# Summing the squares of all six norms by TensorE products in four groups of 32 rows

## The chip, the cores and the metric

The kernel runs on one core of one Trainium2 chip. The metric is the device time of one execution in microseconds. The core has TensorE (products into PSUM), VectorE, ScalarE, GpSimd and SyncE, which issues nearly all transfers; each takes its own queue in order, and they wait for each other by semaphores.

## The reference

Two layers on 1024 tokens with 1024 channels, cut to what matters here. Each layer first takes the root-mean-square norm of a token over its channels and modulates it; the convolution layer also has a LayerNorm over channels inside. All of these need a sum of squares over the channels of each token.

```python
def _rms(x, g):
    xf = x.astype(jnp.float32)
    y = xf * lax.rsqrt(jnp.mean(xf * xf, axis=-1, keepdims=True) + EPS)
    return (y * g.astype(jnp.float32)).astype(x.dtype)

# layer 0 (convolution module), layer 1 (multi-scale pooling mixer); for each:
sh, sc, gt = jnp.split((s_lat @ w_mod[i] + b_mod[i])[:, None, :], 3, axis=-1)
h = _rms(x, norm_g[i]) * (1.0 + sc) + sh
x = x + gt * mixer(h)
# layer 0:  a, b, g = split(h @ w_in);  y = depthwise_conv31(a * sigmoid(b)) + db
#           y = silu(_layernorm(y)) * silu(g);  return y @ w_out
# layer 1:  v, g = split(h @ w_in);  y = grouped(window_means(v) - v) * scale
#           return (y * silu(g)) @ w_out
```

## The kernel before

Activations lie channels by tokens: a channel tile is 128 partitions, and the 1024 tokens are two halves of 512 columns (`h` = 0, 1). A half thus has eight tiles of 128x512. Weights and activations of the large products are split into a high and a low part (`load_split`, `hi_part`, `lo_part`, L162 to L198), and `mm3` (L200) makes three products per tile, with one accumulation over eight tiles in a PSUM bank (`gemm`, L208).

The stages in program order are: norm of x for each half (`norm_x`, L327) with the adaLN vectors of layer 0 made on VectorE between them (`mod_block`, L344); the input products of layer 0 and their gates (`pf`, `pg`, `ps`); adaLN vectors of the rest by `gemv` (L291); the depthwise convolution with 31 taps, per channel tile and half, either on VectorE (L484) or as ScalarE products and GpSimd adds (L471, L472; `POOL_CT` lists GpSimd's tiles: two of eight in the first half, five of eight in the second); the gate products `psg` (L511); the LayerNorm of a half (`layernorm`, L529); the gating (`gate_norm`, L548); the output products `pso` with the residual (`out_half`, L575), which also forms the norm of the second layer (`h2_half`, L606); and layer 1 (`psv`, `psq`, `psy`, `psf`) in two parts.

Six norms sum squares over channels: x0, x1 (the inputs of layer 0), z0, z1 (the variance in the LayerNorm) and y0, y1 (the inputs of layer 1); the digit is the half. Two ways are in use:

- `squares` (L252), for x0, x1 and y1: ScalarE squares a tile (L259, L262), VectorE adds it into one 128x512 total (L266), and `rstd_rows` then sums the partitions of the total by four products, each with a 128x128 block of it as weights and one column of ones streamed (L234). For y1 the last tile is not added but goes through four products of its own.
- `square_sums` (L270), for z0, z1 and y0: ScalarE squares a tile (L275), and four products per tile add it into the four columns of a bank (L277).

Both leave the sums of 512 tokens as 128 partitions by 4 columns. `rstd_rows` (L225) then takes the mean and adds eps on ScalarE (L240), raises to -1/2 on GpSimd (L242), spreads each column into a diagonal on ScalarE (L247, four) and sums the diagonals with ones in one product (L248, `rb`), so that each partition holds the factor of each token. `sq` is a ring of two tiles for the squares.

The order on each engine is set by a planner that runs while the kernel is built: it takes instructions by priority as a simulated timeline makes them ready. `priority(-LATER)` puts a step ahead of all that is not marked so, `LATER * (1 + h)` puts the conv taps behind. `behind(...)` holds a step back in the queue until a named one has been queued; `gemm` uses it to keep a part of its products for the time in which a norm is on its way.

A float32 product appears in the trace as two loads of weights and two multiplies, so the four products of a tile are 8 and 8 instructions.

Of the kernel before, what the change touches and what calls it, by code (L numbers as in the profile page):

```python
# [9 lines left out]
F32 = mybir.dt.float32  # L10
F32R = mybir.dt.float32r
AF = mybir.ActivationFunctionType
# [41 lines left out]
def hybrid_kernel(ctx, tc, xT, vecs, wm, wk, cv_first, cv_w, cv_wo, pl_w, pl_grp, pl_wo, out):  # L54
# [3 lines left out]
    PS = ctx.enter_context(tc.tile_pool(name="ps", bufs=1, space=bass.MemoryType.PSUM))  # L58
    DR = ctx.enter_context(tc.tile_pool(name="dr", bufs=1, space=bass.MemoryType.DRAM))

    RINGS = {"w": 4, "raw": 4, "sg": 2, "sq": 2, "pr": 2, "vs": 1}
    WIDTH = {"E": 2 * NB, "Z": 2 * (NB + 2 * PAD), "sg": NB + 2 * PAD, "pr": NB}
    LATER = 1 << 20
    tc.cur_priority = 4 * LATER
# [31 lines left out]
    def axps(name):  # L96
        return bank("ax", name)
# [4 lines left out]
    def bl(j):  # L102
        return slice(j * P, (j + 1) * P)
# [118 lines left out]

    power_done, spread_done = [None], [None]

    def rstd_rows(total, name):  # L225


        sums, vp = total
        if vp is None:
            vp = axps(f"vp{name}")  # L230
            with priority(-LATER):
                for i, summed in enumerate(sums):
                    for j in range(4):
                        nc.tensor.matmul(  # L234
                            vp[:, j : j + 1], summed[:, bl(j)], ones[:, 0:1], start=i + j == 0,
                            stop=i == len(sums) - 1, skip_group_check=True,
                        )
        ve = S.tile([P, 4], F32, tag="ve", name=f"ve{name}", bufs=2)
        with priority(-LATER):
            nc.scalar.activation(ve, vp[:, 0:4], AF.Identity, scale=1.0 / D, bias=eps)  # L240
        rs = S.tile([P, 4], F32, tag="vr", name=f"vr{name}", bufs=2)
        power_done[0] = nc.gpsimd.tensor_tensor(out=rs, in0=ve, in1=mhalf[:, 0:4], op=ALU.pow)  # L242
        rb = axps(f"rb{name}")
        dg = half("sq", f"dg{name}")
        with priority(-LATER):
            for j in range(4):
                spread = nc.scalar.activation(dg[:, bl(j)], ident, AF.Copy, scale=rs[:, j : j + 1])  # L247
            done = nc.tensor.matmul(rb, ones, dg, start=True, stop=True)  # L248
        spread_done[0] = spread
        return rb, done  # L250

    def squares(xs, name, apart=False):  # L252

        total = half("vs", f"va{name}")
        sums = [total]

        def add(i):
            if i == 0:
                nc.scalar.activation(total, xs[i], AF.Square)  # L259
                return None  # L260
            sq = half("sq", f"sq{name}{i}")
            nc.scalar.activation(sq, xs[i], AF.Square)  # L262
            if apart and i == KT - 1:
                sums.append(sq)
                return None
            return nc.vector.tensor_tensor(out=total, in0=total, in1=sq, op=ALU.add)  # L266

        return (sums, None), add

    def square_sums(xs, name, vp):  # L270


        def add(i):
            sq = half("sq", f"sq{name}{i}")
            done = nc.scalar.activation(sq, xs[i], AF.Square)  # L275
            for j in range(4):
                nc.tensor.matmul(  # L277
                    vp[:, j : j + 1], sq[:, bl(j)], ones[:, 0:1], start=i + j == 0, stop=i == KT - 1,
                    skip_group_check=True,
                )  # L280
            return done

        return (None, vp), add

    def dot(w, out):

# [38 lines left out]
            load_next(xs[h][kt], xT[bl(kt), hs(h)])  # L325

    def norm_x(h):  # L327
        total, add = squares(xs[h], f"x{h}")
        for kt in range(KT):
            last = add(kt)  # L330
        return last, rstd_rows(total, f"x{h}")[0]
# [243 lines left out]
    def out_half(h, y1, ws, done, beside=None):  # L575
        group = len(ws)
        x1 = packed([f"Z{j}" for j in range(4)], f"xr{h}")
        for m in range(KT):
            nc.sync.dma_start(out=x1[m], in_=xT[bl(m), hs(h)])
        total, add = squares(x1, f"y{h}", True) if h else square_sums(x1, f"y{h}", axps("vpy0"))  # L580

        def finish(m, ps):
            nc.vector.scalar_tensor_tensor(  # L583
                out=x1[m], in0=ps, scalar=gt0[:, m : m + 1], in1=x1[m], op0=ALU.mult, op1=ALU.add
            )
            nc.sync.dma_start(out=x1d[m][:, hs(h)], in_=x1[m])
            add(m)

        pss = [mmps(f"pso{h}{m}") for m in range(group)]
        for i, kt in enumerate(CORD):  # L590
            for m in range(group):
                mm3(pss[m], cut(ws[m], bl(kt)), y1[i], i == 0, i == KT - 1)
        for m in range(group):
            finish(m, pss[m])
        for m in range(group, KT):
            with behind([] if m >= group + 2 else done if h == 0 else power_done):
                w = load_split(cv_wo[m], f"wo{h}{m}", eng=(nc.vector, nc.gpsimd)[h])
            if beside is not None:
                beside(m)
            ps = mmps(f"pso{h}{m}")  # L600
            for i, kt in enumerate(CORD):
                mm3(ps, cut(w, bl(kt)), y1[i], i == 0, i == KT - 1)
            finish(m, ps)
        return x1, total
# [279 lines left out]
```

## Time and profile before

| | us |
|---|---|
| median of 3 runs | 758.52 (757.62 to 759.13) |
| the profiled execution | 758.71 |
| its span, first to last instruction | 756.9 |
| TensorE busy | 724.2 (96%) |
| VectorE busy | 532.1 (70%) |
| ScalarE busy | 386.4 (51%) |
| GpSimd busy | 435.4 (58%) |
| chain that ended last | TensorE 70%, VectorE 14%, GpSimd 8%, ScalarE 3% |

PE is TensorE's multiplying, PEld its loading of weights, DVE VectorE, ACT ScalarE, POOL GpSimd, SPq the transfers that SyncE issues. The shares are averages over the whole span; what a stage is limited by is read from its own windows. "PEclk" is the clock granted to TensorE, as a share of 2.4 GHz.

### The profile page before, as it was taken

Reading aid. Unit: us, or ns where it says so; the run is one execution under the profiler, and the core shown is the slowest. Engines: PE = TensorE matmul, PEld = TensorE weight load, DVE = VectorE, ACT = ScalarE, POOL = GpSimd, SP = SyncE. Lnnn points to the kernel's source line nnn. Section 1 sums busy time; section 2 is a strip of 40 time slices with the busy share of each in tenths; the row PEclk is TensorE's granted clock in tenths of the full one; section 3 lists DMA queues with packets and bytes.
Section 4 is the critical chain, followed back from the end, with each engine's and each line's share of the span. In section 5 each row is a group of like instructions: output and inputs, shape, how many; then the busy total and the mean of one; then the engine's idle time right before and its main releaser. Section 6 shows DMA issues by size and latency. Waiting matters only on the chain.

```text
span 756.9 us, 9894 instructions
## 1 busy us (share of the span) xinstructions
PE 724.2 (96%) x3572; PEld 574.1 (76%) x3572; DVE 532.1 (70%) x724; ACT 386.4 (51%) x576; POOL 435.4 (58%) x377
## 2 busy tenths in 40 slices
PE   3899999999999999999989989999999999999998
PEld 1677786676768788778766768788888788888997
DVE  5997997889898941589969989671737364477321
ACT  5355556656613346876886676652414433334110
POOL 2000889999913438899998999763117413344232
PEclk9999999999999999999999989999999999999999
DMA  8882006466323441643650132445625610334132
GB/s 324 315 318 82 0 1 249 167 223 233 132 82 98 152 153 63 202 140 113 207 171 24 57 126 83 154 168 160 203 92 203 200 56 28 98 112 140 56 126 72
DMA packets 36481, 105.68 MB, mean 140 GB/s; under 512 B 4048, under 2 KB 6224, under 8 KB 36432
## 3 DMA queue, kind: packets, MB, share of 16 engines
q1 hardware_dynamic: 36432, 105.05, 40.8%
q8 instruction: 28, 0.46, 0.2%
q14 instruction: 21, 0.17, 0.1%
HBM read 92.45 MB, written 12.58 MB: 139 GB/s over the span
## 4 chain that ended last, share of the span: by engine, by line
PE 70%; DVE 14%; POOL 8%; ACT 3%; issue 2%; DMA 2%; SPq 0%; DVEq 0%; POOLq 0%; ACTq 0%
POOL z L472 8%; PE ps L201 4%; PE ps L203 4%; PE ps L202 4%; PE psf L202 4%; PE psf L203 4%; PE psf L201 4%; PE psv L203 3%; PE psv L202 3%; PE psv L201 3%; PE psq L202 3%; PE psq L201 3%; PE psq L203 3%; PE psg L203 3%; PE psg L201 3%; PE psg L202 3%
## 5 line engine op out<-in xcount | busy, mean ns | idle before, releaser
L472 POOL TENSOR_TENSOR z<-z,pr 128x512 f32<-128x512 f32 (+8 forms) x210 | 297.1, 1415 | 49.4 <-ACT pr L471 21.2
L471 ACT ACTIVATE pr<-y,VT 128x512 f32<-128x512 f32 (+8 forms) x210 | 150.2, 719 | 96.8 <-POOL z L472 90.2
L484 DVE SCALAR_TENSOR_TENSOR cv<-y,VT,cv 128x512 f32<-128x512 f32 (+12 forms) x261 | 175.4, 741 | 0.4
L770 DVE SCALAR_TENSOR_TENSOR xf<-psf,gt,xf 128x260 f32<-128x260 f32 (+1 forms) x24 | 13.2, 570 | 36.9 <-PE psf L203 31.4
L753 DVE SCALAR_TENSOR_TENSOR q<-psy,VT,q 128x260 f32<-128x260 f32 (+1 forms) x24 | 13.6, 571 | 31.9 <-PE psy L203 31.7
L242 POOL TENSOR_TENSOR vrx<-vex,mhalf 128x4 f32<-128x4 f32 x2 | 2.1, 1026 | 57.2 <-ACT vex L240 57.2
L567 DVE TENSOR_TENSOR z<-z,rbz 128x512 f32<-128x512 f32 x16 | 10.7, 680 | 28.9 <-PE rbz L248 28.9
L671 DVE TENSOR_TENSOR s<-v 128x535 f32<-128x535 f32 x8 | 12.3, 1536 | 19.5 <-ACT v L719 19.5
L675 DVE TENSOR_TENSOR s<-s 128x517 f32<-128x517 f32 (+5 forms) x24 | 20.9, 870 | 0.6
L559 ACT ACTIVATE gn<-z,VT 128x512 f32<-128x512 f32 x16 | 12.4, 777 | 14.6 <-DVE z L567 14.4
L287 DVE SCALAR_TENSOR_TENSOR wmb<-wmb,s_row 128x1024 f32<-128x1024 f32 x16 | 19.4, 1220 | 0.0
L583 DVE SCALAR_TENSOR_TENSOR xr<-pso,gt,xr 128x512 f32<-128x512 f32 x16 | 11.5, 741 | 10.7 <-PE pso L203 10.7
L299 PE MATMUL gv<-wk,srep 128*32 128x256 f32 x256 | 18.6, 388 | 0.0
L164 ACT CAST y<-q 128x504 fp32r<-128x504 f32 (+1 forms) x16 | 9.9, 618 | 16.8 <-DVE q L753 16.8
L169 DVE TENSOR_TENSOR y<-q,y 128x504 fp32r<-128x504 f32 (+1 forms) x16 | 13.9, 869 | 3.6 <-ACT y L164 3.6
L277 PEld LDWEIGHTS vpz<-ones,sqz 128*128 128x128 f32 x128 | 15.5, 191 | 0.7
L275 ACT ACTIVATE sqz<-z 128x512 f32<-128x512 f32 x16 | 9.8, 629 | 12.0 <-PE vpz L277 11.5
L202 PE MATMUL psy<-pd,grs 128*128 128x260 f32 (+1 forms) x48 | 15.3, 320 | 0.0
L203 PE MATMUL psy<-pd,grs 128*128 128x260 f32 (+1 forms) x48 | 15.3, 319 | 0.0
L201 PE MATMUL psy<-pd,grs 128*128 128x260 f32 (+1 forms) x48 | 15.1, 318 | 0.0
L277 PE MATMUL vpz<-ones,sqz 128*128 128x1 f32 x128 | 14.7, 245 | 0.0
L169 DVE TENSOR_TENSOR grs<-gr,grs 128x512 fp32r<-128x512 f32 x8 | 9.1, 1132 | 8.0 <-ACT grs L164 8.0
(2503 smaller groups left out, 2352.6 us busy)
## 6 DMA issues: line engine op xcount, KB each, us to landing
wk<-in_wk SPq DMA_DIRECT2D x32, 512.0 KB, 5.1
wmb<-in_wm SPq DMA_DIRECT2D x16, 512.0 KB, 6.4
wo<-in_cv_wo SPq DMA_DIRECT2D x16, 512.0 KB, 3.5
wp<-in_pl_wo SPq DMA_DIRECT2D x16, 512.0 KB, 3.5
wg<-in_cv_w SPq DMA_DIRECT2D x12, 512.0 KB, 3.7
wv<-in_pl_w SPq DMA_DIRECT2D x12, 512.0 KB, 3.4
wq<-in_pl_w SPq DMA_DIRECT2D x12, 512.0 KB, 3.5
x<-in_xT SPq DMA_DIRECT2D x16, 256.0 KB, 6.2
```

Of the source, the lines that this page charges most:

```text
L169: return eng.tensor_tensor(out=lo, in0=src, in1=hi.bitcast(F32), op=ALU.subtract)
L201: nc.tensor.matmul(ps, w[0], r[0], start=first, stop=False)
L202: nc.tensor.matmul(ps, w[0], r[1], start=False, stop=False)
L203: nc.tensor.matmul(ps, w[1], r[0], start=False, stop=last)
L277: nc.tensor.matmul(vp[:, j : j + 1], sq[:, bl(j)], ones[:, 0:1], start=i + j == 0, stop=i == KT - 1, skip_group_check=True,)
L287: nc.vector.scalar_tensor_tensor(out=w, in0=w, scalar=1.0, in1=s_row, op0=ALU.mult, op1=ALU.mult, accum_out=out)
L299: nc.tensor.matmul(ps[32 * q : 32 * q + 32, :256], srep[:, kt, :], w[:, 256 * q : 256 * q + 256], start=kt == 0, stop=kt == KT - 1,)
L471: nc.scalar.activation(pr[:, o], y[:, i], AF.Copy, scale=dw(k))
L472: nc.gpsimd.tensor_tensor(out=z[:, o], in0=z[:, o], in1=pr[:, o], op=ALU.add)
L484: nc.vector.scalar_tensor_tensor(out=a[:, o], in0=y[:, i], scalar=dw(k), in1=a[:, o], op0=ALU.mult, op1=ALU.add)
L675: nc.vector.tensor_tensor(out=s[:, :m], in0=s[:, :m], in1=s[:, step : step + m], op=ALU.add)
L753: mixed[0] = nc.vector.scalar_tensor_tensor(out=sg[m][:, piece], in0=ps, scalar=vcol(ct, V_PS), in1=sg[m][:, piece], op0=ALU.mult, op1=ALU ...
```

## The change

All six norms sum their squares by products, tile by tile, and `squares` with its total is gone. The product is turned round: a constant block of 32 columns, `onesd` (1/1024), is the weights, and the 128 columns of a quarter of the tokens are streamed; quarter j writes rows 32j to 32j+31 of the bank, so the four sums of 128 tokens stand as rows. `rstd_rows` copies these 128x128 values with eps added, turns them into 128x4 by a product with `sel` (one 1 in each of rows 0, 32, 64 and 96), and copies these 4 columns; the power is now inside the priority block.

```diff
-    RINGS = {"w": 4, "raw": 4, "sg": 2, "sq": 2, "pr": 2, "vs": 1}
+    RINGS = {"w": 4, "raw": 4, "sg": 2, "sq": 2, "pr": 2}
...
-    def rstd_rows(total, name):
-        sums, vp = total
-        if vp is None:
-            vp = axps(f"vp{name}")
-            with priority(-LATER):
-                for i, summed in enumerate(sums):
-                    for j in range(4):
-                        nc.tensor.matmul(
-                            vp[:, j : j + 1], summed[:, bl(j)], ones[:, 0:1], start=i + j == 0,
-                            stop=i == len(sums) - 1, skip_group_check=True,
-                        )
-        ve = S.tile([P, 4], F32, tag="ve", name=f"ve{name}", bufs=2)
+    def token_sums(ps, src, first, last):
+        for j in range(4):
+            nc.tensor.matmul(ps[32 * j : 32 * j + 32, :P], onesd[:, :32], src[:, bl(j)], start=first, stop=last)
+
+    def rstd_rows(vp, name):
+        row = S.tile([P, P], F32, tag="vrow", name=f"vrow{name}", bufs=1)
+        rs = S.tile([P, 4], F32, tag="vr", name=f"vr{name}", bufs=2)
         with priority(-LATER):
-            nc.scalar.activation(ve, vp[:, 0:4], AF.Identity, scale=1.0 / D, bias=eps)
-        rs = S.tile([P, 4], F32, tag="vr", name=f"vr{name}", bufs=2)
-        power_done[0] = nc.gpsimd.tensor_tensor(out=rs, in0=ve, in1=mhalf[:, 0:4], op=ALU.pow)
+            nc.scalar.activation(row, vp[:, :P], AF.Identity, bias=eps)
+            nc.tensor.matmul(vp[:, P : P + 4], row, sel, start=True, stop=True)
+            ve = S.tile([P, 4], F32, tag="ve", name=f"ve{name}", bufs=2)
+            nc.scalar.copy(ve, vp[:, P : P + 4])
+            power_done[0] = nc.gpsimd.tensor_tensor(out=rs, in0=ve, in1=mhalf[:, 0:4], op=ALU.pow)
...
-    def squares(xs, name, apart=False):
...
     def square_sums(xs, name, vp):
         def add(i):
             sq = half("sq", f"sq{name}{i}")
             done = nc.scalar.activation(sq, xs[i], AF.Square)
-            for j in range(4):
-                nc.tensor.matmul(
-                    vp[:, j : j + 1], sq[:, bl(j)], ones[:, 0:1], start=i + j == 0, stop=i == KT - 1,
-                    skip_group_check=True,
-                )
+            token_sums(vp, sq, i == 0, i == KT - 1)
             return done
-        return (None, vp), add
+        return vp, add
...
     def norm_x(h):
-        total, add = squares(xs[h], f"x{h}")
+        total, add = square_sums(xs[h], f"x{h}", axps(f"vpx{h}"))
...
-        total, add = squares(x1, f"y{h}", True) if h else square_sums(x1, f"y{h}", axps("vpy0"))
+        total, add = square_sums(x1, f"y{h}", axps(f"vpy{h}"))
```

## Rows read from the trace of the kernel before

**Rows 1.** The page: a busy line and TensorE's forty slices, in tenths.

```profile
PE 724.2 (96%) x3572; PEld 574.1 (76%) x3572; DVE 532.1 (70%) x724; ACT 386.4 (51%) x576; POOL 435.4 (58%) x377
...
PE   3899999999999999999989989999999999999998
```

**Rows 2.** Windows of 10 us: length, PE, PEld, DVE, ACT, POOL busy; PEclk; DMA.

```profile
40.00:50.00 10.00, 9.44 (x40) 7.35 (x41) 9.99 (x20) 5.62 (x9) 0.00 (x0) 1.00 1.04 411
440.00:450.00 10.00, 6.26 (x25) 4.76 (x24) 9.44 (x10) 7.80 (x13) 9.69 (x11) 0.85 0.32 104
```

**Rows 3.** Timeline, TensorE, first burst of y0 (start, us, engine, line, operation, count).

```profile
337.54 0.39 PE L202 MATMUL pso<-y102l,wo04h 128*128 128x512 f32 x1
337.77 1.84 PE L277 MATMUL vpy<-ones,sqy 128*128 128x1 f32 x16
...
339.79 0.40 PE L201 MATMUL pso<-y102h,wo04h 128*128 128x512 f32 x1
```

**Rows 4.** Timeline, TensorE, last burst of y0.

```profile
372.44 0.39 PE L202 MATMUL psg<-h12l,wg61h 128*128 128x512 f32 x1
372.67 0.95 PE L277 MATMUL vpy<-ones,sqy 128*128 128x1 f32 x8
...
373.80 0.39 PE L201 MATMUL psg<-h14h,wg61h 128*128 128x512 f32 x1
```

**Rows 5.** The chain that ended last: first burst of z0, last of z1.

```profile
268.22 1.68 PE vpz L277 x16
...
522.84 1.68 PE vpz L277 x16
```

**Rows 6.** Timeline, TensorE, first burst of the adaLN vectors.

```profile
122.50 0.40 PE L203 MATMUL ps<-h04h,wb4l 128*128 128x512 f32 x1
122.83 0.64 PE L299 MATMUL gv<-wk,srep 128*32 128x256 f32 x8
...
123.74 0.39 PE L202 MATMUL ps<-h04l,wb4h 128*128 128x512 f32 x1
```

**Rows 7.** Timeline, TensorE, channel sums of the first LayerNorm (some records are missing).

```profile
225.16 0.39 PE L203 MATMUL ps<-h16h,wb7l 128*128 128x512 f32 x1
225.47 1.92 PE L537 MATMUL mr<-z,onesd 128*32 128x512 f32 x14
...
227.65 0.39 PE L202 MATMUL ps<-h10l,wa7h 128*128 128x512 f32 x1
```

**Rows 8.** Window of 40 ns, adaLN instructions only (length; PE, PEld busy and count).

```profile
122.87:122.91 0.04, 0.04 (x4) 0.04 (x8) 0.00 (x0) 0.00 (x0) 1.00 0.50 205
```

**Rows 9.** Instructions of the adaLN tile: duration in ns, least, median, most.

```profile
L299 PEld LDWEIGHTS gv<-wk,srep x256: 106/109/110, 122.8 to 214.4; 128*32 128x32 f32 x128
```

**Rows 10.** Timeline, TensorE, two turning products of an adaLN vector.

```profile
141.51 0.39 PE L202 MATMUL ps<-h16l,wb4h 128*128 128x512 f32 x1
141.74 0.50 PE L308 MATMUL gv<-sel,row 128*128 128x4 f32 x4
...
142.43 0.39 PE L201 MATMUL ps<-h10h,wa4h 128*128 128x512 f32 x1
```

**Rows 11.** VectorE's adds for x0 and x1 (tile view); TensorE's timeline at 75.

```profile
L266 DVE TENSOR_TENSOR vax<-vax,sqx x14: 682/690/693, 6.8 to 57.4; 128x512 f32<-128x512 f32 x14
...
75.35 0.50 PE L202 MATMUL pg<-h10l,w00h 128*128 128x512 f32 x1 [1.16 <-DVE h10l L170]
```

**Rows 12.** ScalarE's diagonal blocks of the x norms (tile view, ns).

```profile
L247 ACT ACTIVATE dgx<-ident,vrx x8: 387/387/402, 17.2 to 64.2; 128x128 f32<-128x128 f32 x8
```

**Rows 13.** Timeline, TensorE, spreading product of y0; idle before it in brackets.

```profile
382.49 1.13 PE L248 MATMUL rby<-dgy,ones 128*128 128x512 f32 x2 [0.74 <-ACT dgy L247]
```

**Rows 14.** Timeline, ScalarE and GpSimd: conv taps of the second half, start and end.

```profile
282.15 0.63 ACT L275 ACTIVATE sqz<-z 128x512 f32<-128x512 f32 x1 [4.17 <-PE vpz L277]
...
285.07 2.66 POOL L472 TENSOR_TENSOR z<-z,pr 128x512 f32<-128x512 f32 x2 [13.47 <-ACT pr L471]
...
484.68 3.96 POOL L472 TENSOR_TENSOR z<-z,pr 128x499 f32<-128x499 f32 x3
```

More of the change, by code (lines that the diff above doesn't have):

```diff
@@ L250, in rstd_rows @@
         return rb, done
-    def squares(xs, name, apart=False):
[L254 to L268, printed above, removed]
     def square_sums(xs, name, vp):
```

## The prediction

> **What bounds the kernel now.** I read the busy shares and the forty slices first: TensorE is busy in nearly every slice, VectorE, ScalarE and GpSimd are not [rows 1]. So a saved microsecond counts where TensorE is the one behind, and I looked for the stretches where it is not. In the windows TensorE has small gaps near the front, where VectorE is full, and one of 3.7 us near 445, with a lower clock in that window (0.85) [rows 2]. Everywhere else I treat TensorE time as the time of the kernel. Then I read, on TensorE's own timeline, what each way of summing squares costs.
>
> **The price of the old products.** A sum by `ones[:, 0:1]` loads a 128x128 block of squares as weights and streams one column, four times for one channel tile. Ordinary products start every 0.23 us, so a burst's price is the distance between the starts of its neighbours, less two ordinary steps (0.46). Two tiles in one burst: 337.54 to 339.79 is 2.25, less 0.46, 1.79 us [rows 3]. One tile: 372.44 to 373.80, 1.36 less 0.46, 0.90 us [rows 4]. Both z norms run as four bursts of two tiles, eight bursts in all, of which the first and the last stand in [rows 5]; y0 runs as two bursts of two and four of one, of which [rows 3, 4] show one each. x1 has one burst of one tile's size after VectorE has added its eight squares; y1 has two, because its last tile is kept apart.
>
> **The price of the new products.** The new form keeps `onesd[:, :32]` as weights and streams 128 columns of squares, four times, into four groups of 32 rows. No row of before has just this, but two neighbours differ only in columns. The adaLN products stream 256 columns into the four groups: 122.50 to 123.74 is 1.24, less 0.46, 0.78 us for one set of four [rows 6]. The channel sums of the LayerNorm stream 512 columns, two sets in a burst: 225.16 to 227.65 is 2.49, less 0.46, 2.03 us [rows 7]. The difference, 1.25 us over 1024 - 256 = 768 columns, is 1.63 ns a column and leaves 0.36 us that does not depend on columns. For 128 columns I take 0.36 + 0.21 = 0.57 us for one tile and 0.36 + 0.42 = 0.78 for two in a burst. The lower end is the 0.21 alone, if the fixed part is hidden; the upper end is 0.78 a tile, the row of 256 columns, if a set pays for its eight loads and eight multiplies and not for columns. I stay with the line through both, as in the 40 ns from 122.87 four multiplies and eight loads of the adaLN burst are in flight (the counts in brackets) [rows 8], so instructions do not queue one behind another.
>
> One rule speaks against this. The adaLN loads of 32 columns take 0.109 us each [rows 9], yet they overlap [rows 8]. The Trainium skill, "TensorE: Matmul & The Clock Gate", section "The mechanism" (of Part 3), says that a load of weights overlaps a running product only when it goes to another group of rows; the four sets here share all rows. This case's trace does not agree for groups of columns: eight loads are in flight beside four multiplies in 40 ns. What the rule would do is the last rival.
>
> **The change part by part.**
> - z0 and z1: four bursts each go from 1.79 to 0.78, -4.0 us. Each norm now also turns its rows back into a column: one product with `sel` after a 128x128 copy. Two such products cost 141.51 to 142.43, 0.92 less 0.46, 0.46 us [rows 10]; for one I take 0.3 (0.23 to 0.46). So -3.7 each.
> - y0: 2 x (0.78 - 1.79) + 4 x (0.57 - 0.90) + 0.3 = -3.0.
> - y1: was 2 x 0.90; becomes eight sets. Its tiles finish as y0's do, so 2 x 0.78 + 4 x 0.57 = 3.8, with 0.3 and less 1.8: +2.3. Its six VectorE adds go, but TensorE is full there [rows 1], so I price them at nothing; if they did hold up something, that would be a gain.
> - x1: was one burst, 0.90; becomes eight sets, 8 x 0.57 = 4.6, +0.3: +4.0 on TensorE. In return seven adds of 0.69 us leave VectorE [rows 11] in a stretch where VectorE is full (9.99 of 10) and TensorE lacks 0.56 of 10 [rows 2], and TensorE's wait of 1.16 at 75 for the first tile of the second half [rows 11] should go, as its norm is done earlier. I count these 1.7 us back: +2.3. Each set waits for its square on ScalarE, and TensorE takes its queue in order, so a late square holds up the products of `pf` queued behind it; the ring of two squares is now freed by TensorE and not by VectorE. Ends: +0.8 if the sets pair up, +4.0 if no gap closes.
> - x0: TensorE is idle this early; VectorE's last two adds (2 x 0.69) leave the chain and a copy, a product and another copy enter it. 0, ends -1.4 and 0.
> - The chain behind each norm gets a 128x128 activation, the product and a second copy in place of one small activation: about 0.9 us, an estimate: 0.39 us for a 128x128 ScalarE block [rows 12], 0.3 for the product, the rest for the second copy. ScalarE, GpSimd (the power) and the queue of TensorE (the spreading product) wait for it. At z0, z1 and x1 other products fill that time. At y0 TensorE already waits 0.74 us for that chain [rows 13], so there 0.9 counts. The power also moves ahead in GpSimd's queue, past GpSimd's share of weight splits and conv taps that are not yet started; a tap is 1.3 us, so this takes back at most that at y0 and I count nothing.
>
> **Does the gain reach the end?** Up to 299 the path is TensorE. From 285 to 488.6 GpSimd adds conv taps with hardly a pause [rows 14], and the second LayerNorm needs its last one. It starts when ScalarE, held by squares that wait 4.17 us for the products [rows 14], gets to the taps. Three bursts stand ahead of that point, so GpSimd starts 3 x 1.0 us earlier, less x1's +2.3: -0.7 at 489. By TensorE and VectorE the same point moves by 2.3 - 3.7 - 3.0 + 0.9 = -3.5. Which of them is late depends on how the queue interleaves; between -0.7 and -3.5 I take the middle, -2.1. After that TensorE is full again: z1 -3.7, y1 +2.3. Sum: -2.1 - 1.4 = -3.5 us. The profiled execution has 758.71 us (span 756.9 and 1.8 around it), the median is 758.52; 758.5 - 3.5 = 755.0. With the ends of x1 and of the middle above, its own range is 753 to 757. About 0.2% (1.5 us) is what a measurement here can tell from no change.
>
> **Rivals.**
> - All of TensorE's saving arrives: x1's sets pair up (+0.8), GpSimd does not hold up the second LayerNorm and y0's longer chain is covered. 0.8 - 3.7 - 3.0 - 3.7 + 2.3 = -7.3, 751.2. For it: full slices after 490. Against: GpSimd's unbroken row of taps.
> - Spent on the way: x1 costs its full +4.0, GpSimd sets the point at 489 (4.0 - 3.0 = +1.0), and z1 and y1 give -1.4: -0.4, 758.1, no change to be seen. For it: TensorE has almost no gap to give at the front.
> - Slower: a set of four pays by instruction. At the 0.78 of the adaLN row, and 1.20 for two, z0 and z1 give -2.1 each, y0 -1.4, y1 costs +4.0 and x1 +3.9: +2.3, 760.8. The five norms that matter hold 40 sets, 12 pairs and 16 singles, against 24.2 us of old bursts; with five turning products (1.5) and 1.7 of gaps closed it breaks even at 0.72 us a set, and above that the change loses, since x1 and y1 had cheap sums before. Against: the counts in flight, and the price falling with columns.
> - Slower by far: the loads of the four column groups run one by one, 8 x 0.109 + 0.21 + 0.36 = 1.44 us a set (two in a burst 2.5). By the same count 40 x 1.44 - 4.3 - 24.2 + 1.5 - 1.7 = +28.9, 787. The rule of the Trainium skill named above would do this; the burst of before speaks clearly against it.
>
> **How the numbers follow.** Forecast 0.48, full saving 0.17, spent on the way 0.18, by instruction 0.15, loads one by one 0.02. The likeliest gives 755.0. The range takes in the full saving, with a little more for an early x0, and the price by instruction: 750.5 to 761.0; it leaves out the last case. Faster: nearly all of the first and all of the second, 0.63. Same: 0.19. Slower: 0.18. The range also has room for the low-clock stretch near 445 going or another coming, which no step here decides.
>
> **What would show it.** A burst of one new set should stand 1.0 to 1.1 us between its neighbours' starts (0.57 + 0.46); 1.24 or more means price by instruction. The last z0 burst should end some 3 us earlier against its first, and the first conv tap of the second half on GpSimd with it. TensorE's gaps up to 80 should shrink, and the product into the second half's first tile should not wait. The distance from the last GpSimd tap to the end should shrink by 1 to 2 us. The forecast is wrong if the sets of x1 make TensorE wait for ScalarE in its queue, or if the new order opens a long TensorE gap between 300 and 490.

## The result and the profile after

The changed kernel takes 770.43 us (median; 767.85 to 771.22), the kernel before, measured beside it, 758.07. The ratio is 1.0156, with a 95% interval from 1.0128 to 1.0183: slower by 12.4 us, where 755.0 was forecast. The profiled execution is of 770.67 us, its span 768.9.

The busy line and two of the forty-slice rows of the page of the changed kernel, to be set against [rows 1]:

```profile
PE 727.0 (95%) x3744; PEld 560.6 (73%) x3744; DVE 513.5 (67%) x704; ACT 388.1 (50%) x582; POOL 432.8 (56%) x377
...
PE   3899899999999999889889979999999899999998
...
PEclk9799999999999999999989989999999999999999
```

VectorE has lost 18.6 us of work (532.1 to 513.5); its 20 adds, now gone, took 20.4. TensorE's own time is nearly the same (724.2 to 727.0). The span grew by 12.0 us, and 9.2 of them are TensorE's empty time (32.7 to 41.9).

**The sums cost what was forecast.** TensorE's timeline around one burst of two sets in z0, then around one of a single set in y0 (start, duration, engine, line, operation, count). They answer [rows 3, 4]:

```profile
280.51 0.40 PE L201 MATMUL psg<-h10h,wg20h 128*128 128x512 f32 x1
280.84 0.64 PE L229 MATMUL vpz<-sqz,onesd 128*32 128x128 f32 x16
...
281.75 0.39 PE L203 MATMUL psg<-h10h,wg20l 128*128 128x512 f32 x1
...
348.17 0.40 PE L202 MATMUL pso<-y100l,wo05h 128*128 128x512 f32 x1
348.50 0.43 PE L229 MATMUL vpy<-sqy,onesd 128*32 128x128 f32 x8
...
349.19 0.39 PE L201 MATMUL pso<-y100h,wo05h 128*128 128x512 f32 x1
```

280.51 to 281.75 is 1.24, less two ordinary steps of 0.23, 0.78 us for a pair; 348.17 to 349.19 gives 0.56 for one. The forecast had 0.78 and 0.57. (x16 stands for the eight products of two sets: TensorE writes two row entries for a product of type fp32.)

**Time goes to the waits behind the norms.** TensorE at the first tile of the second half, which answers [rows 11]; the wait before it stands in brackets, and the next rows start 0.43 us apart where 0.23 is usual:

```profile
80.34 0.75 PE L202 MATMUL pg<-h10l,w00h 128*128 128x512 f32 x1 [3.68 <-DVE h10l L170]
80.89 0.63 PE L203 MATMUL pg<-h10h,w00l 128*128 128x512 f32 x1
81.32 0.63 PE L201 MATMUL pg<-h10h,w01h 128*128 128x512 f32 x1
```

The wait of 1.16 us that was to go has become one of 3.68. Windows of 10 us show the others (columns as in [rows 2]; behind z0, and around the spreading products of y0 and y1). First the kernel before:

```profile
310.00:320.00 10.00, 10.00 (x43) 7.51 (x41) 5.92 (x10) 8.75 (x15) 8.86 (x8) 1.00 0.61 195
320.00:330.00 10.00, 8.29 (x33) 5.54 (x33) 7.29 (x11) 8.41 (x13) 9.15 (x7) 1.00 0.16 56
...
380.00:390.00 10.00, 9.18 (x37) 6.41 (x35) 4.98 (x5) 8.44 (x15) 9.32 (x7) 1.00 0.60 197
...
600.00:610.00 10.00, 10.00 (x43) 7.87 (x43) 6.76 (x9) 6.00 (x10) 5.83 (x3) 1.00 0.27 84
```

Then the change, in which these stretches come some 4 to 12 us later:

```profile
310.00:320.00 10.00, 8.46 (x35) 5.64 (x33) 6.40 (x11) 9.38 (x16) 8.43 (x7) 1.00 0.54 180
320.00:330.00 10.00, 7.50 (x29) 4.61 (x27) 5.68 (x9) 8.86 (x15) 9.37 (x9) 1.00 0.33 109
...
390.00:400.00 10.00, 6.98 (x23) 4.64 (x22) 3.34 (x5) 7.74 (x15) 9.22 (x7) 0.83 0.45 165
610.00:620.00 10.00, 7.35 (x26) 5.26 (x25) 4.62 (x7) 5.40 (x11) 3.84 (x3) 0.83 0.18 54
```

So part of the emptiness behind z0 is old: the waits in front of `pso` products add up to 1.7 us there before (310 to 335) and to 5.2 in the change (311 to 336).

And this is the chain of y0 from its last set of sums to its spreading product, on all engines; the last line answers [rows 13]:

```profile
379.48 0.43 PE L229 MATMUL vpy<-sqy,onesd 128*32 128x128 f32 x8 [0.93 <-ACT sqy L255]
385.44 0.36 ACT L236 ACTIVATE vrowy<-vpy,eps 128x128 f32<-128x128 f32 x1
389.29 0.28 PE L237 MATMUL vpy<-sel,vrowy 128*128 128x4 f32 x2
390.34 0.14 ACT L239 COPY vey<-vpy 128x4 f32<-128x4 f32 x1
391.34 1.02 POOL L240 TENSOR_TENSOR vry<-vey,mhalf 128x4 f32<-128x4 f32 x1
393.47 1.26 ACT L245 ACTIVATE dgy<-ident,vry 128x128 f32<-128x128 f32 x4
394.78 2.07 PE L246 MATMUL rby<-dgy,ones 128*128 128x512 f32 x2 [3.02 <-ACT dgy L245]
```

The steps' own times are as expected: 0.36, 0.28, 0.14 us. But the copy starts 5.5 us after the sums end, the turning product 3.5 us after the copy, the second copy 0.8 us after that: each stands in its engine's queue behind work that was put there earlier (ScalarE's casts and conv taps, TensorE's ordinary products). The first of these waits is not new. In the kernel before the last set ends at 373.62 [rows 4], and ScalarE's small activation starts 5.2 us after it:

```profile
378.84 0.24 ACT L240 ACTIVATE vey<-vpy,eps 128x4 f32<-128x4 f32 x1
```

From the last set to the spreading product y0 takes 15.3 us (9.8 before, from [rows 4] to [rows 13]); of the 5.5 us more, 4.7 are the turning product and the second copy with the waits in front of them. TensorE waits 3.02 us for the spreading product, where it waited 0.74.

### The profile page after: what moved, and what is told of

The parts are those of the page before. It is cut to its first block, busy times and chain, and to the rows that moved or that the text cites. A ratio compares the mean times of both kernels' runs of the same rounds, so it can differ in the third digit from the quotient of the medians.

```text
span 768.9 us, 10222 instructions
## 1 busy us (share of the span) xinstructions
PE 727.0 (95%) x3744; PEld 560.6 (73%) x3744; DVE 513.5 (67%) x704; ACT 388.1 (50%) x582; POOL 432.8 (56%) x377
## 4 chain that ended last, share of the span: by engine, by line
PE 77%; POOL 9%; DVE 5%; ACT 4%; issue 3%; DMA 2%; SPq 0%; POOLq 0%; ACTq 0%
POOL z L448 8%; PE ps L201 4%; PE ps L203 4%; PE ps L202 4%; PE psf L202 4%; PE psf L203 4%; PE psv L203 4%; PE psf L201 4%; PE psv L201 4%; PE psv L202 4%; PE psg L201 3%; PE psg L202 3%; PE psg L203 3%; PE psq L203 3%; PE psq L201 3%; PE psq L202 3%
## 5 line engine op out<-in xcount | busy, mean ns | idle before, releaser
L729 DVE SCALAR_TENSOR_TENSOR q<-psy,VT,q 128x260 f32<-128x260 f32 (+1 forms) x24 | 13.6, 570 | 29.8 <-PE psy L203 29.6
L651 DVE TENSOR_TENSOR s<-s 128x517 f32<-128x517 f32 (+5 forms) x24 | 25.5, 1062 | 0.6
L647 DVE TENSOR_TENSOR s<-v 128x535 f32<-128x535 f32 x8 | 12.3, 1538 | 19.5 <-ACT v L695 19.5
L590 DVE SCALAR_TENSOR_TENSOR xr<-xr,a,rby 128x512 f32<-128x512 f32 x16 | 11.6, 737 | 14.1 <-PE rby L246 14.1
L535 ACT ACTIVATE gn<-z,VT 128x512 f32<-128x512 f32 x16 | 12.3, 774 | 13.2 <-DVE z L543 13.2
L275 PE MATMUL gv<-wk,srep 128*32 128x256 f32 x256 | 18.6, 388 | 0.0
L201 PE MATMUL psy<-pd,grs 128*128 128x260 f32 (+1 forms) x48 | 15.1, 318 | 0.0
L465 DVE TENSOR_TENSOR z<-z,cv 128x512 f32<-128x512 f32 x9 | 6.1, 683 | 11.8 <-ACT z L464 11.8
L456 DVE TENSOR_SCALAR cv<-y,VT 128x512 f32<-128x512 f32 (+1 forms) x18 | 12.8, 748 | 1.3 <-ACT z L464 1.3
```

The source lines that it names most:

```text
L201: nc.tensor.matmul(ps, w[0], r[0], start=first, stop=False)
L275: nc.tensor.matmul(ps[32 * q : 32 * q + 32, :256], srep[:, kt, :], w[:, 256 * q : 256 * q + 256], start=kt == 0, stop=kt == KT - 1,)
L651: nc.vector.tensor_tensor(out=s[:, :m], in0=s[:, :m], in1=s[:, step : step + m], op=ALU.add)
L729: mixed[0] = nc.vector.scalar_tensor_tensor(out=sg[m][:, piece], in0=ps, scalar=vcol(ct, V_PS), in1=sg[m][:, piece], op0=ALU.mult, op1=ALU ...
```

## The experiments

The kernel before was measured beside every run: medians 757.8 to 758.1. "Hop" below means what the change adds to the chain behind a norm: a copy, a product on TensorE and a copy back, in place of one small activation. The diffs are cut to the lines that matter; "..." marks what is left out.

Theory after the result: the hop, by its places in the queues of TensorE and ScalarE, makes the loss, and the sums gain about what was forecast. Rivals: the sets of x1 and y1 (sums that VectorE had done for nothing), and the power's new place in GpSimd's queue.

**Only the hop (e1).** The kernel before, its sums untouched, with a product by the identity and a copy in every chain:

```diff
         rs = S.tile([P, 4], F32, tag="vr", name=f"vr{name}", bufs=2)
+        with priority(-LATER):
+            nc.tensor.matmul(vp[:, P : P + 4], ident, ve, start=True, stop=True)
+            ve = S.tile([P, 4], F32, tag="ve2", name=f"ve2{name}", bufs=2)
+            nc.scalar.copy(ve, vp[:, P : P + 4])
```

> The kernel before with all its sums as they were, and in each of the six norms one more hop in the chain: the four columns pass through a product with the identity and a second copy on ScalarE before the power. Theory of the hop (the added product and copy wait in the queues of TensorE and ScalarE, and everything behind the norm comes late): the changed kernel loses 12.4 us although its sums cost TensorE some 5 us less, so the hop alone costs up to 17; 768 to 776 us. Theory of the sets (x1 and y1 now cost TensorE eight sets each, and moving them reorders the queues): the hop is hidden, 757 to 760. Theory of the power (its move into the priority block): 757 to 760.

Measured: 774.25 us (773.15 to 776.52), ratio 1.0226 [1.0204, 1.0249], +16.5 us for six products and six copies of 0.28 and 0.16 us (x0's product takes 0.56).

**The change without the hop (e2).** The turning product and the 128x128 copy are left out, and one small activation reads the first four columns of the sums; so the factors belong to other tokens, while the sums cost what they do in the change:

```diff
...
-            nc.scalar.activation(row, vp[:, :P], AF.Identity, bias=eps)
-            nc.tensor.matmul(vp[:, P : P + 4], row, sel, start=True, stop=True)
             ve = S.tile([P, 4], F32, tag="ve", name=f"ve{name}", bufs=2)
-            nc.scalar.copy(ve, vp[:, P : P + 4])
+            nc.scalar.activation(ve, vp[:, 0:4], AF.Identity, bias=eps)
```

> The changed kernel with its new sums, but the turning product and the second copy left out: ScalarE reads the first four columns of the rows directly, as before, so the factors belong to other tokens; all other work is there. Theory of the hop: the gain of the sums is seen, 751 to 756 us. Theory of the sets: 766 to 770. Theory of the power (still inside the priority block): 766 to 770.

Measured: 753.57 us (753.4 to 755.54), ratio 0.995 [0.9935, 0.9965]: -4.2 us. The sums gain, those of x1 and y1 included, so the rival of the sets falls. -4.2 and +16.5 make +12.3, and the change lost 12.4.

**The power put back (e3).** The change, with GpSimd's power at its old place in the queue:

```diff
-            power_done[0] = nc.gpsimd.tensor_tensor(out=rs, in0=ve, in1=mhalf[:, 0:4], op=ALU.pow)
+        power_done[0] = nc.gpsimd.tensor_tensor(out=rs, in0=ve, in1=mhalf[:, 0:4], op=ALU.pow)
```

> The changed kernel with the power outside the priority block, as before. Theory of the power: 757 to 762 us. The other two theories: 768 to 772.

Measured: 770.14 us (769.32 to 771.82), the time of the change. That rival falls.

**Sums and hop in z1 alone (e4).** The kernel before; only z1 takes the new sums with their longer chain (a flag `sums == "rows"` selects the change's copy, product and copy):

```diff
...
-        total, add = square_sums(z, f"z{h}", bank(("ax", "cv")[h], f"vpz{h}"))
+        total, add = (row_sums if f"z{h}" in ('z1',) else square_sums)(z, f"z{h}", bank(("ax", "cv")[h], f"vpz{h}"))
...
```

> The kernel before, with the new sums and the longer chain in the second LayerNorm (z1) alone. There TensorE had 4 us of other work between the ready diagonals and the spreading product. Theory of the hop: the hop is covered at this place, the four bursts give 4.0 us less 0.2: 754 to 756 us. Theory of the sets: z1 is not x1 or y1, 754 to 756 too. If even one hop in this place costs more than the sums give, 758 to 762.

Measured: 756.24 us (755.33 to 757.04), ratio 0.9981 [0.9971, 0.999], -1.5 us, just above the 754 to 756 expected. TensorE's time on the sums of z fell by 4.3 us (13.6 to 9.3), so 2.8 of them did not arrive. In the kernel before TensorE was full there; now it is less so (a window of 100 us, columns as above, before and then this run):

```profile
500.00:600.00 100.00, 99.50 (x472) 82.07 (x471) 47.63 (x63) 40.45 (x60) 42.20 (x22) 1.00 0.53 171
...
500.00:600.00 100.00, 97.35 (x481) 77.60 (x480) 51.23 (x63) 40.58 (x64) 42.77 (x23) 1.00 0.50 171
```

Of the 2.8 us, 1.7 stand in one wait, and it is not one for a normalized tile: TensorE waits for the low part of a weight that GpSimd splits (before, then this run). This run does not tell how much of it the hop brought about.

```profile
587.39 0.50 PE L203 MATMUL pso<-y110h,wo17l 128*128 128x512 f32 x1 [0.51 <-POOL wo17l L169]
...
585.00 0.50 PE L203 MATMUL pso<-y110h,wo17l 128*128 128x512 f32 x1 [2.23 <-POOL wo17l L169]
```

**The price of the hop by place (e12, e13, e14).** e1's hop in two of the six norms at a time; the diff is that of e12, and e13 names 'y0' and 'y1', e14 'z0' and 'z1':

```diff
+        if name in ('x0', 'x1'):
             with priority(-LATER):
                 nc.tensor.matmul(vp[:, P : P + 4], ident, ve, start=True, stop=True)
...
```

> The kernel before, with the additional product (by the identity) and the additional copy in the chain of the two x norms alone. Theory (each place has its own price, read from TensorE's time by tile in the kernel with six such hops: the first tiles behind the x norm +5.1 us, the spreading product +2.7): +6 to +8 us, 764 to 766. Rival (a hop costs the same everywhere, 16.5 / 6 = 2.75 us each): +5 to +6, 762.5 to 763.8. Rival (what is lost here is given back at a later wait): under +3.

> The kernel before, with the additional product and copy in the chain of the two y norms alone. Theory (by place: the products of psg behind the first y norm +5.5 us, the wait in front of the second y norm's additional product +3.2): +8 to +9 us, 766 to 767; the two z norms are then left with 0 to 3 of the 16.5. Rival (the same everywhere): +5 to +6, 762.5 to 763.8.

> The kernel before, with the additional product and copy in the chain of the two z norms alone. The prediction put this at nothing, because at the z norms other products fill the time: 757.5 to 758.3. The two runs before (both x norms +7.4, both y norms +5.0) leave 4.1 of the six hops' 16.5, if places add up: +3 to +5.5, 761 to 763.5.

Measured: x norms 765.25 us (764.11 to 766.15), ratio 1.0098 [1.0083, 1.0112], +7.4; y norms 762.9 (762.65 to 766.58), 1.0079 [1.0056, 1.0102], +5.0; z norms 761.87 (761.34 to 764.21), 1.0052 [1.0035, 1.007], +3.8. Together 16.2 of e1's 16.5, so the places add up. No place is free. For y the median is that of the equal split and not the +8 to +9 that I had read from e1's trace; three of its four runs lie at 762.65 to 763.11 and one, the traced one, at 766.58. At x1 the added length arrives whole: in e12 the spreading product starts at 72.01, 5.35 us later than before (66.66), and TensorE's waits for the first tiles of the second half are 2.08 and 4.38 us instead of 1.16, 5.3 more. In e14 the extra product of z0 and its spreading product are, on TensorE:

```profile
285.80 1.81 PE L282 MATMUL vpz<-ones,sqz 128*128 128x1 f32 x15
292.17 0.28 PE L244 MATMUL vpz<-vez,ident 128*128 128x4 f32 x2
300.21 1.02 PE L253 MATMUL rbz<-dgz,ones 128*128 128x512 f32 x2
318.02 0.50 PE L201 MATMUL pso<-y102h,wo00h 128*128 128x512 f32 x1 [0.99 <-ACT y102h L164]
321.43 0.50 PE L201 MATMUL pso<-y102h,wo00h 128*128 128x512 f32 x1 [1.01 <-ACT y102h L164]
```

Other products do fill the 14.4 us between the sums and the spreading product (11.7 before). TensorE waits later, at 318 and 321, for tiles that are made from the normalized z: in the kernel before the wait that stands in their place is

```profile
320.35 0.50 PE L201 MATMUL pso<-y102h,wo00h 128*128 128x512 f32 x1 [0.33 <-ACT y102h L164]
```

**Queue position at x1 (e9).** The change; the products of channel tiles 6 and 7 may only be queued behind x1's turning product (in the change 5.3 us of them stand ahead of it):

```diff
...
                 for kt in range(KT - LAST, KT):
-                    mm3(pf[n, ct], wfirst(kt, n, ct), hT[0][kt], False, kt == KT - 1)
+                    with behind(turn_done):
+                        mm3(pf[n, ct], wfirst(kt, n, ct), hT[0][kt], False, kt == KT - 1)
```

> The change, but the products of channel tiles 6 and 7 of the first group, which in the change are queued on TensorE between the last set of sums of the second half's x norm and its turning product (59.0 to 64.5 us), are queued behind that turning product. Nothing else differs in the source. TensorE then waits some 1 us at 59, for the row copy, and the chain of this one norm loses about 4 us of queue. Theory (queue position): the spreading product and all that follows come 3 to 6 us earlier, 764 to 768 us, and the wait of 3.7 us at 80 goes. Rival (the length of the chain's work, not its place): 769.5 to 772, the 1 us wait added.

Measured: 767.65 us (766.13 to 769.6), ratio 1.0123 [1.0108, 1.0139]; -2.8 against the change. The chain has the same steps and pays one wait of 0.48 us for its place at the front. Its spreading product starts at 66.87 instead of 71.92, and the wait of 3.68 us at 80 is gone. TensorE's rows in e9:

```profile
58.26 0.64 PE L230 MATMUL vpx<-sqx,onesd 128*32 128x128 f32 x14
59.37 0.39 PE L238 MATMUL vpx<-sel,vrowx 128*128 128x4 f32 x2 [0.48 <-ACT vrowx L237]
66.87 1.02 PE L247 MATMUL rbx<-dgx,ones 128*128 128x512 f32 x2
```

So the place in the queue counts, not the work, though the gain itself is small beside the spread of the runs (the intervals of the change and of e9 overlap); e10 below shows the same more clearly. Of the 5 us won at 71.92 some half reached the end; the y0 stretch waited longer (5.0 us of one product at 384.74, start to next start, where the longest there in the change was 3.4 at 391.37).

**The turn on VectorE (e8).** The change's sums in all six norms, but the turn is a multiplication by a 0/1 mask and a sum over groups, both on VectorE; the diagonals are then written with a stride:

```diff
...
-            nc.scalar.activation(row, vp[:, :P], AF.Identity, bias=eps)
-            nc.tensor.matmul(vp[:, P : P + 4], row, sel, start=True, stop=True)
-            nc.scalar.copy(ve, vp[:, P : P + 4])
+            nc.vector.scalar_tensor_tensor(out=tmp, in0=vp[:, :P], scalar=EPS, in1=mask, op0=ALU.add, op1=ALU.mult)
+            nc.vector.tensor_reduce(ve, tmp.rearrange("p (r c) -> p c r", c=4), mybir.AxisListType.X, ALU.add)
...
```

> The change, but the turn is done by VectorE instead of by TensorE and ScalarE: one instruction adds eps to the 128 sums of each row and multiplies by a 0/1 mask that keeps four of them (partition 32j+r keeps tokens 128j+4r to 128j+4r+3), a second sums over groups to 128 x 4; then the same power, four scaled diagonals (with a stride of 4 columns) and the same spreading product. Full result. Same number of steps in the chain as in the change, but none of them in TensorE's queue. Theory (the hop costs by its place in TensorE's queue): 753 to 758, within 0.6 % of the kernel with no turn. Rival (the hop costs by the two additional instructions wherever they stand): 766 to 771.

Measured: 757.24 us (755.98 to 758.41), ratio 0.999 [0.9981, 0.9999]; -13.2 against the change, with a chain that has one instruction less and no turn on TensorE or ScalarE. It leaves open which of the three counts most. That the sums stand as rows does not make the loss, as they do so here too. VectorE's queue is not free either: at y0 the first step starts 3.2 us after the sums end and the second 1.4 us after the first, and the chain takes 11.4 us there (372.98 to 384.34; 15.3 in the change, 9.8 before). In x1 they follow each other at once:

```profile
63.00 0.29 DVE L244 SCALAR_TENSOR_TENSOR vrowx<-vpx,mask 128x128 f32<-128x128 f32 x1 [3.55 <-PE vpx L236]
63.32 0.38 DVE L245 TENSOR_REDUCE vex<-vrowx 128x4 f32<-128x128 f32 x1
63.78 1.01 POOL L246 TENSOR_TENSOR vrx<-vex,mhalf 128x4 f32<-128x4 f32 x1 [47.52 <-DVE vex L245]
```

**No turn, a long power (e7).** The sums stay as 128 columns; GpSimd takes the power of all of them, and four products pick the rows, so product, second copy and diagonals go:

```diff
...
+        power_done[0] = nc.gpsimd.tensor_tensor(out=row, in0=row, in1=mhalf[:, 0:1].broadcast_to((P, P)), op=ALU.pow)
...
             for j in range(4):
-                spread = nc.scalar.activation(dg[:, bl(j)], ident, AF.Copy, scale=rs[:, j : j + 1])
-            done = nc.tensor.matmul(rb, ones, dg, start=True, stop=True)
+                done = nc.tensor.matmul(rb[:, bl(j)], pick[:, j, :], row, start=True, stop=True)
```

> The change, with the same sums by four groups of columns, but the chain behind them has no turning product and no copy: ScalarE adds eps to the 128 sums of each row (as in the change), GpSimd raises all 128 columns to the power -1/2 in one instruction (in the change 4 columns), and four 128-column products with a 0/1 matrix that picks row 32j for quarter j spread the factors; ScalarE's four diagonal tiles (4 x 0.39 us) go too. Full result. Theory (the extra hop through TensorE's queue made the loss): the result is that of the kernel with no turn, 753.6 us, less up to 1.5 us per norm for the diagonals where nothing else fills that time, plus the longer power: 750 to 757, faster than the kernel before by 0.1 to 1 %. Rival (the row form of the sums itself costs, because the kernel with no turn read other tokens' columns and so also left out the row copy): 762 to 771. Rival (power of 128 columns is long on GpSimd, over 5 us): 757 to 765, with the power seen as the chain's longest step.

Measured: 866.57 us (865.63 to 867.07), ratio 1.1434 [1.1418, 1.1449], outside all three expectations. The groups by line have the cause (count, busy us, mean ns):

```profile
L240 POOL TENSOR_TENSOR vrowx<-vrowx,mhalf 128x128 f32<-128x128 f32 x2 | 42.0, 20986 | 58.5 <-ACT vrowx L239 58.5
```

21.0 us instead of the 1.02 of the 128x4 power; I had allowed for "over 5". It is no test of the turn, but it is one of the chain: each of six powers got about 20 us longer and the kernel 113 us slower than e2, some 19 a norm. (GpSimd's conv taps also wait for these powers, and TensorE's granted clock was 0.92; this run does not tell these apart.)

**What is left at x1, and a version faster than both (e10, e11).** e10 is e8 with the products of tiles 6 and 7 queued behind x1's last set, the edit of e9 with another step to wait for. e11 is the kernel before with the new sums and the VectorE turn in z0, z1 and y0 only; both x norms and y1 keep their VectorE sums. The edit of e10 against e8, then that of e11 against the kernel before:

```diff
...
-                    mm3(pf[n, ct], wfirst(kt, n, ct), hT[0][kt], False, kt == KT - 1)
+                    with behind(sums_done):
+                        mm3(pf[n, ct], wfirst(kt, n, ct), hT[0][kt], False, kt == KT - 1)
...
-        total, add = square_sums(z, f"z{h}", bank(("ax", "cv")[h], f"vpz{h}"))
+        total, add = (row_sums if f"z{h}" in ('z0', 'z1', 'y0') else square_sums)(z, f"z{h}", bank(("ax", "cv")[h], f"vpz{h}"))
...
```

> The kernel with the turn on VectorE (mask and sum over groups), with one thing more: the products of channel tiles 6 and 7 of the first group are queued on TensorE behind the last set of sums of the second half's x norm, instead of in part ahead of it. Full result. Theory (what is left of the loss at x1 is that its sums are queued behind other products, so the spreading product comes 3 to 4 us later than before, TensorE waits 3.2 us for the first tile of the second half and then runs 3 us at half clock): that wait goes, as it did with the queue change made on the change itself (-2.8 us): 752.5 to 754.5 us. Rival (the time regained at 80 us is lost again in the waits of TensorE at 371 to 384 or 440 to 474 us): 756.5 to 758.

> The kernel before, with the new sums and the VectorE turn only in the three norms where the kernel before already summed on TensorE (both z norms and the first y norm); both x norms and the second y norm keep their sums on VectorE. Full result. Theory, from TensorE's time by tile (from the start of each product to the start of the next): the sums of z take 13.6 us before and 5.1 with the new sets, those of y0 some 3 less, 11 us in all; less what the mask's two instructions add to three chains, up to 1 us each: 747 to 751. Rival (the waits later on grow by what the sums give, as the waits at 371 to 384 and 442 to 474 do in the kernel with six masked norms): 753 to 757.

Measured: e10 751.13 us (750.94 to 752.22), ratio 0.9917 [0.9903, 0.9931]; e11 748.93 (748.49 to 749.59), ratio 0.9884 [0.987, 0.9898]. e10 came out below its range: one edit in the order of TensorE's queue is worth 6.1 us in e8. Its x1 chain starts 5 us earlier than e8's,

```profile
58.12 0.29 DVE L246 SCALAR_TENSOR_TENSOR vrowx<-vpx,mask 128x128 f32<-128x128 f32 x1 [1.39 <-PE vpx L237]
...
66.42 1.02 PE L256 MATMUL rbx<-dgx,ones 128*128 128x512 f32 x2
```

and no wait for the second half's first tile is left. e11 is the fastest: it takes the sums where TensorE paid for them already and leaves x and y1 alone.

Where TensorE's time went, all in one table. It is worked out from the timelines: the time from each product's start to the next one's, added up by the tile that the product writes, in us (a burst's neighbours hold up to 0.2 us of it):

| tile | what it is | before | e2, no hop | change | e9 | e8, mask | e11 |
|---|---|---|---|---|---|---|---|
| vpz | sums of z0, z1 | 13.6 | 5.2 | 4.9 | 4.9 | 5.1 | 5.1 |
| vpy, rby | sums and spread of y0, y1 | 9.4 | 6.6 | 10.8 | 10.3 | 6.6 | 5.4 |
| vpx, rbx, ps_s, pf | the x norms and what lies between | 62.2 | 62.0 | 65.0 | 65.0 | 63.6 | 61.8 |
| pg | products behind x1 | 52.2 | 56.7 | 55.9 | 50.0 | 55.8 | 52.1 |
| pso | products behind z0 | 92.8 | 93.7 | 98.2 | 98.2 | 93.7 | 93.2 |
| psg | products up to and behind y0 | 94.2 | 96.6 | 101.4 | 102.1 | 96.5 | 96.7 |
| psv, psq | products of the second half's gates | 189.6 | 188.6 | 188.7 | 189.9 | 189.3 | 189.2 |
| psf | last products | 91.3 | 92.9 | 92.8 | 94.2 | 93.6 | 92.4 |

The column of the change against that of e2: pso +4.5, psg +4.8, vpy and rby +4.2, the x norms +3.0, and -0.8 for pg. That is the hop's 15 us, place by place (the traced executions of the two differ by 15.1), and of it only about 6 x 0.23 = 1.4 us are the hop's own products.

## Why the prediction was wrong, point by point

- **TensorE bounds the kernel, a saved microsecond of its work counts.** Right for the work that was taken off, and only half of the matter. The prediction treated TensorE time as the kernel's time and so read the path as a sum of products. TensorE takes its products in order, and what it lost were waits, for the spreading products and for the tiles behind the norms: 28.9 us of waits before, 28.1 in e2, 38.1 in the change.
- **Prices of the sums.** Right: 0.78 and 0.56 measured against 0.78 and 0.57. z0 and z1 ran as four pairs each, vpz fell by 8.8 us (8.0 forecast). y0 came as one pair and six singles (two and four forecast) and y1 as eight singles. The price by instruction (0.78 a set) and the loads one by one (1.44 a set) fell with it. The Trainium skill, "TensorE: Matmul & The Clock Gate", section "The mechanism" (of Part 3), says that a load of weights overlaps running products only when it goes to another group of rows. For groups of columns on the same rows the trace of the change does not agree: 16 row entries of 0.27 us each stand within 0.64 us.
- **The total of the sums.** Right in size, in part by luck: -4.2 without the hop, where the same sum without its 0.3 for each turning product and 0.9 for the longer chain gives some -5 (the forecast of -3.5 held both). Its parts were not right. The second LayerNorm's last channel sum (the mark at 489) was to come 2.1 us earlier; in e2 it comes 4.4 later (493.8 against 489.4), GpSimd's last conv tap 4.6, and the rest of the kernel gives 7.5. Other products had moved across that mark (behind it stand 218 products into `psq` in e2, 240 before), so it was no place at which a sum could be split.
- **x1: the wait of 1.16 at 75 should go, +2.3.** Wrong even without the hop. In e2 the wait is 3.21 us, 13 products behind it start 0.43 us apart, and the adaLN vectors begin 4.3 us later than before (127.1 against 122.8). VectorE's adds did go, and the diagonals are ready a little earlier; but their spreading product, placed behind more of TensorE's ordinary products, starts 2.1 us later, and the wait is longer by as much. The rows of the kernel before, then of e2 (the wait of before is in [rows 11]):

```profile
63.29 1.28 ACT L247 ACTIVATE dgx<-ident,vrx 128x128 f32<-128x128 f32 x4 [1.12 <-POOL vrx L242]
66.66 1.02 PE L248 MATMUL rbx<-dgx,ones 128*128 128x512 f32 x2
...
62.92 1.28 ACT L242 ACTIVATE dgx<-ident,vrx 128x128 f32<-128x128 f32 x4
68.75 1.02 PE L243 MATMUL rbx<-dgx,ones 128*128 128x512 f32 x2
77.17 0.80 PE L202 MATMUL pg<-h10l,w00h 128*128 128x512 f32 x1 [3.21 <-DVE h10l L170]
```

  e9 and e10 show that the order of the queue is the cause: with the fillers behind the turn or the sums the spreading product starts at 66.87 and 66.42, and the wait goes.
- **"The chain behind each norm ... about 0.9 us ... At z0, z1 and x1 other products fill that time."** This is the step that failed; it holds nearly all of the miss. The work was priced well (0.36, 0.28 and 0.14 us at y0, 0.8 in all). Two things were left out. First, each new step is a new place in an in-order queue: at y0 the turning product stands 3.5 us behind TensorE's products and the second copy 0.8 behind ScalarE's work. Second, cover at the spreading product is not cover: the products that fill the wait are finished earlier, and TensorE then waits at the products that need a normalized tile (at 80 for x1, from 312 to 327 for z0). At y0 and y1 the cover runs out: TensorE waits at the spreading product itself (until 394.78 and 613.13). Forecast: 0.9 at y0, nothing at the others. Measured with the kernel before and a hop alone: +7.4 at the x norms, +5.0 at the y norms, +3.8 at the z norms. y1, which the prediction's item on the chain did not list, waits too: its spreading product has 2.65 us of idle time before it, and none in the kernel before.
- **VectorE's adds at y1 at nothing.** Not shown: no run takes them away alone.
- **The power moved ahead.** Rightly counted at nothing (e3).
- **The rivals.** None of them held the mechanism. Both that ended slower priced the sums, and the range up to 761.0 came from the nearer one; a rival "a step added to a chain that crosses engines waits in each queue, at all six norms" was missing, though the row of y0's wait [rows 13] and that at 75 [rows 11] were its first signs: both showed TensorE already waiting for such a chain, so that an added length could be expected to arrive, as it did at x1 in e12.
- **What would show it.** The text named "a long TensorE gap between 300 and 490" and a wait for the second half's first tile as signs that the forecast is wrong. Both came. Of the signs that it is right one came, the distance around a single set (1.02 us). The last z0 burst was to end some 3 us earlier against its first and ended 0.8 earlier (20.6 us before, 19.8 in the change and in e2), as more ordinary products stand between the bursts; the stretch from GpSimd's last tap to the end grew by 3.6 us instead of shrinking.

What stays open: why the y norms' hops cost 5.0 us alone where e1's tiles showed some 9, and why one of the four runs with them lost 8.7. In e1 other places (psv, psq) gained 5 us at the same time, so a row by tile is not a price; only the runs by place are. The planner orders all queues anew for every edit, so each price holds the new order too, and no run keeps the order fixed. The lower clock can be counted only roughly: products of 128x512 that start 0.40 to 0.46 us apart number 13 before, 29 in e2 and 35 in the change. At 0.2 us each, an estimate, that is 4.4 us of the change against before, but 1.2 of it against e2.

## What to carry to other kernels

Price a step that is added to a chain across engines by its places in the in-order queues, not by its length: here a product and a copy of 0.28 and 0.16 us cost 1.9 to 3.7 us a norm (3.8 to 7.4 for two), and the turn on VectorE 0.6 (757.24 against 753.57, over six). Products that fill a wait can postpone it to the first product that needs the late tile, as at x1 and z0; ask whether TensorE already waits for that chain anywhere, and if it does, count all of an added length there. When the sums are cheap and the way to them dear, change the order of the queue first: one such edit gave 6.1 us.

## What the runs showed of the hardware that was not expected

- GpSimd's power grows with the columns: 1.02 us for 128x4 and 20.99 for 128x128 in e7, on average 161 ns for each added column (20.99 less 1.02, over 124; two sizes only, and e7 reads its exponent from one column).
- Products into four groups of columns are in flight together (16 row entries of 0.27 us within 0.64 us), and the price of such a set of 128 columns (0.56) lay on the line drawn through 256 and 512 columns.
- A wait of TensorE can cost more than its length. After 3.68 us without a product seven of the next started 0.43 us apart instead of 0.23 (1.4 us more), and the granted clock of that window (80 to 90) was 0.83, part of it at the lower of the two levels, 1.2 GHz; after y0's wait of 3.02 us (0.83 from 390 to 400) the spreading product took 2.07 us, before 1.13 [rows 13]. After the waits of about 1 us at 324 and 327 the clock stayed 1.00.
